# An early one-column activation on ScalarE and two new tables of order in a two-block kernel

## The chip, the cores and the metric

The kernel runs on one core of a Trainium2 chip. The metric is the device time of one execution in microseconds. The core has five engines, which run their own instruction streams and meet through semaphores: TensorE (PE: matmuls, and the loads of its stationary operand as PEld), VectorE (DVE), ScalarE (ACT), GpSimd (POOL) and SyncE (SP, which here only issues DMA transfers). ACT issues a few transfers too.

## The reference

256 tokens of width 1024, all in fp32, go through two blocks, one after the other, batch 1. Cut to what matters:

```python
# first block, on 16 meta tokens + 256 tokens (272 rows)
u = rmsnorm(h, g_pre_mix)
q, k, v, xr, yr = split(u @ w_in)
attn = sliding_window_attention_with_sinks(q, k, v, sinks)   # 8 heads, window 128
hr = rg_lru(causal_depthwise_conv(xr, conv_w, conv_b), ...)  # a gated linear recurrence
mix = concat([attn, gelu(yr) * hr]) @ w_out
h = h + rmsnorm(mix, g_post_mix)
u = rmsnorm(h, g_pre_ffn)
h = h + rmsnorm(square(relu(u @ w_ff1)) @ w_ff2, g_post_ffn)
# second block, on the 256 tokens
proj = rms_norm(h, ln_pre_mix) @ w_in_2                      # q, k, v, qkv_b, z, b, a, gates
y_a = moba_attention(rope(q), rope(k), v)                    # 8 heads of 128
y_b = rms_norm(gated_delta_rule(...)) * silu(z)              # 8 heads of 128
merged = sigmoid(gate_a) * (y_a @ w_proj_a) + sigmoid(gate_b) * (y_b @ w_proj_b)
h = h + rms_norm(merged @ w_out_2, ln_post_mix)
f = rms_norm(h, ln_pre_ffn)
h = h + rms_norm((silu(f @ w_ffn_gate) * (f @ w_ffn_up)) @ w_ffn_down, ln_post_ffn)
h = h + sigmoid(h @ w_ple_gate) * rms_norm(p @ w_ple, ln_ple)
```

The norms, attentions and recurrences are small. Most of the work is products with weight matrices, some 145 MB of them, each read once.

## The kernel before, in words

**Products in three.** A weight tile is 128 rows by 1024 columns of fp32, loaded by SP into a buffer called `raw` (four of them; `weight_dma`, L208). It is split in two halves of 512 columns (`prep`, L218 on): `whi` is the value rounded to the type that PE multiplies fast, `wlo` the rest, `raw` less `whi`. The activations are split the same way (`uT`, `mgT`, `hm`). A product is three matmuls, hi by hi, hi by lo and lo by hi (`mm3`). The rounding copy is one instruction on ACT or on DVE (`copy`: L174 on ACT, L172 on DVE), and the subtraction is one on DVE (L178). There are 258 weight tiles, so some 516 half splits. Groups of three matmuls follow one another on PE, and as long as the splits are ahead of them PE waits for nothing.

**The order of work.** Each engine runs its instructions in the order in which the Python code emits them. PE's matmuls are emitted by a list of jobs. Between groups of matmuls a job calls `tick()`, which counts steps and looks the number up in the table `ORDER_OF_WORK`: at that step a `p` emits one half split, and a name emits the next step of a generator of that name ("side"): `first` and `rest` are the splits and the x tiles of the start, `stats` and `rms` the first norm, `attn0` to `attn3`, `lru0` to `lru3` and `gdn0` to `gdn3` pieces of attention, recurrence and delta rule, `norm10` to `norm41` the norm boundaries between the parts (`norm30` and `norm31` for token rows 0 to 127 and 128 to 255 at the third of them). A second table, `VECTOR_COPIES`, lists for each stream (`m` for the jobs, `p12` for weight tile 12, or a side's name) which of its rounding copies go to DVE; the rest go to ACT. The two tables are data: no rule of the kernel derives them.

**The start.** DVE fills `warm`, `mhalf` and `ones` with constants (L540 to L542). PE multiplies `warm` with itself 20 times while the first transfers run. SP issues the first x tile (`xT`, four of them, two chunks of 128 features each) and the halves of the first two weight tiles; ACT issues `gc`, the gains of the first norm, 4 KB (L585). For each of eight chunks `x_prep` scales x by its gain on ACT (L576, the high part of `uT`) and takes the low part on DVE (L577). `part(i, j)` splits half j of weight tile i: (0,0) at once, then (1,0), (0,1) and (1,1) by the side `first`. The first job uses tiles 0 and 1: for each of the eight chunks three matmuls with tile 0 and three with tile 1, 48 in all.

**A norm boundary.** Each half (512 features) of the product in PSUM is squared and summed on ACT (L300), multiplied by the gain on DVE (`m`, L463), scaled by the norm and added to the residual `h` (L469). From `h` the next norm's `u` is made (L480), PE transposes it in blocks of 128 (L324), and ACT and DVE split the transposed half into two `uT` (L174, L178).

Of the kernel before, what the change touches and what calls it, by code (L numbers as in the profile page):

```python
# [56 lines left out]
10:stats,stats,p,stats,stats,p,stats,stats 11:p,stats,p 12:p 22:p 27:rms,rms 29:xr1*2 32:kv0*2,p,p 38:p,p 42:xr0*2
47:p 52:p,xr2*2 60:p 63:q0*2,xr3*2,p,p 64:p 73:lru1,lru2 77:kv1*2 78:attn0 80:lru0,lru1 81:vtok,attn1,lru3,lru3
86:attn0,p,lru1,p,p,p,p,p 87:attn1 90:q1*2 91:lru3 107:lru3 116:attn0 119:attn1 123:y0*2 125:attn2 126:lru3
132:attn0,attn3 133:rec0*2 135:p,rms 136:attn1,attn0*2 138:p 139:p,p 141:attn3 142:p,p,p 143:attn2,attn2 144:attn1*2  # L60
148:attn3 150:spill,y1*2 153:attn2 157:p,spill,attn2*2 166:p,p,p,p,p,p,attn3,p,p,rec1*2 171:rec0,attn3*2
173:p,p,p,rec1 182:p,p,p 192:p 196:p,p,p 202:norm10*2,p 204:norm10*2,norm10,norm10,norm10 208:norm11*2 212:norm10
218:norm11*2,norm11 219:norm10,norm10 221:norm11 224:p 226:norm11,norm11,norm11 228:norm11,p,p,p,p 235:p,p 244:p,p
254:p,p 257:hma0 261:hma1 279:p 281:p,p,p 285:p 295:p,p,p,p,p,p,p,p 319:p 340:p,p,p,p,p,p,p 342:spill 348:p,p 379:p,p
396:p 414:p,p,p,p,p,p 417:p,p,p,p,p 418:p 431:p,p 477:p 480:p 488:p,p,p,p,p,p,p 502:p 516:p 519:p,p 528:p,p,p,p,p,p
532:p 541:p,p 552:p 560:p 562:p,p 587:p,p,p 610:p 631:p,p,p,p,p 634:p,p,p,p,p 664:p,p,p 677:p 685:p,p 721:spill
729:p,p,p,p 732:p,p,p,p 735:p,p 739:p 766:p,p 783:p 789:p,p 803:p 811:p,p 820:p,p 833:p,p,p,p,p,p 849:p,p,p,p,p
871:norm20*2,norm20*2,norm20,norm20 873:norm20,norm20 875:norm21*2 883:norm20 885:norm21*2,norm21 886:norm20,norm21
894:p,norm21,p,norm21 896:p,p,norm21,norm21 900:p,p,p,gates 902:p,p,p,p 905:p,p,p 906:gates 910:p 911:p,p,p,p,p
912:gates 931:p,p,p,p 934:p,p,p 935:gates 940:p 964:p,p,p,p 979:p 992:p,p,p 1002:p,p 1019:p,p 1032:p,moba0 1050:moba1  # L70
1067:p 1068:p,p 1073:p,p 1076:moba1,moba1 1096:gates 1097:p 1100:p 1103:p 1107:moba0 1109:moba0 1110:moba2 1117:p
1125:p,moba1,p,p 1129:moba2 1136:moba2,moba0,moba1 1146:p,p,p 1164:p,p,p,moba3 1171:p,moba2 1191:moba3,moba3 1194:p
1195:p 1213:qkv01,qkv01 1220:p,p,p 1221:p 1223:qkv00,qkv00,qkv00,gates 1227:moba2,p 1233:qkv02,qkv02,gdn0
1243:p,gdn0,gdn0 1246:gdn0,gdn0,gdn0,gdn0,gdn0 1249:p,p,p,p 1259:p,p 1266:gdn0 1269:p 1273:p 1288:p 1292:p,p,p,p,p
1294:moba3 1314:p,p,p 1321:gdn0 1324:gdn0,p 1337:moba0,p 1354:qkv10,qkv10 1359:p,p,p,p,p 1366:gdn0,gdn0 1373:moba3
1379:qkv11,p 1389:p 1393:p,p 1396:qkv11 1405:gdn0 1406:gdn0,gdn0 1422:p,qkv10 1431:p,p,p 1434:qkv12
1435:qkv12,gdn1,gdn1 1440:gdn0 1441:gdn1,gdn1 1444:gdn0,gdn0,gdn1,gdn1 1454:p 1455:p,p,p 1460:qkv21 1466:gdn1
1467:gdn1 1468:gdn0 1484:qkv20,p,gdn0,qkv20,qkv20 1486:gdn0,gdn1 1487:p 1492:gdn1,gdn1,gdn0 1493:qkv22 1496:qkv30
1499:p 1502:gdn0 1503:qkv21 1506:qkv30,p 1515:gdn0 1516:qkv22,gdn2,gdn2 1520:p,gdn0,gdn1 1522:gdn1 1529:gdn0
1533:gdn2,gdn2 1535:qkv31 1536:p,p 1538:gdn0 1555:gdn0,gdn0 1559:qkv31,gdn2,gdn1,gdn1 1561:qkv30  # L80
1568:gdn0,qkv32,qkv32,gdn3,gdn3,gdn2,gdn2,gdn1 1575:p,p,gdn3,gdn2,gdn2,p,p,p,p 1584:p,gdn1 1587:gdn2 1593:gdn1,gdn1
1594:gdn3 1600:gdn1 1603:gdn1 1606:gdn3,gdn3 1607:p,p,p,p,p,p,gdn1,gdn2,gdn3,gdn2,gdn2 1616:gdn1 1627:gdn1 1632:gdn3
1633:gdn1 1639:gdn3,gdn1,p 1645:p,gdn1 1646:gdn2,gdn0,gdn2,gdn2 1658:gdn1 1669:p,p,p,p,p 1671:gdn2
1672:gdn3,p,p,p,gdn1,gdn3,gdn3,gdn3 1678:gdn1,gdn2,gdn2 1685:gdn0*2 1689:gdn1,gdn2 1691:p 1702:gdn2 1704:gdn1
1707:gdn3,gdn3,gdn3 1710:p,p,p,p 1715:gdn1*2,gdn3 1717:gdn2,gdn3,gdn2,p,gdn3 1720:p,gdn2 1731:gdn3 1734:gdn2
1741:p,p,p,p,gdn2 1743:gdn3,gdn2,p,p,p,p 1747:gdn3,p,p 1750:gdn2 1759:gdn3 1760:p 1769:gdn3,gdn2,gdn2 1773:gdn3
1779:gdn3 1783:gdn3 1789:gdn2 1792:gdn3 1793:p 1795:p,p 1796:gdn3 1802:gdn3 1809:gdn3 1811:gdn2,gdn3 1821:gdn2*2,p
1822:p 1825:gdn3*2 1827:p 1834:p,p 1840:p,p,p 1844:p 1848:p,p,p 1856:p 1863:p 1889:p 1909:p 1923:p,p 1932:pb1,pb0
1935:p,p,p 1936:p 1939:p 1942:p,p,pb2 1949:p 1967:p,p,p,p 1974:pb3,p 1976:p,p 1981:p,p 1996:p
2008:norm30*2,norm30*2,norm30,norm30 2018:norm30,norm31*2,norm30 2028:norm31*2,norm31 2029:norm30,norm30 2031:norm31  # L90
2034:p,norm31,norm31 2037:p,p,p,p,norm31,norm31,p,p,p 2047:p,p 2048:p 2054:p,p 2055:p 2056:p,p 2065:p,p 2073:hmb0
2074:hmb1 2081:p 2089:p 2093:p 2103:p 2110:p,p,p,p,p,p,p,p,p 2131:p,p,p,p 2140:p,p 2141:p 2150:p 2182:p,p
2217:p,p,p,p,p,p,p,p 2249:p,p 2252:p,ple 2281:p 2288:p,p,p,p,p 2300:p,p 2317:p,p,p 2319:p 2330:p,p,p 2332:p,p,p
2370:p,p,p,p 2376:p 2383:p,p,p 2392:p 2398:p 2402:p 2413:p,p,p,p 2421:p,p 2444:p,p,p,p 2485:p 2493:p 2501:p
2506:p,p,p,p,p,p 2545:p,p 2553:p,p 2564:p,ple,p,p,p,p 2597:p,p,p,p,p 2612:p,p,p,p 2615:p,p,p 2647:p,p 2654:ple
# [4 lines left out]
VECTOR_COPIES = """  # L100
m:0,2,4,5,8,10,12,13,16,17,18,19,21,23,24,26,27 first:2 p2:0,1 p3:0 p11:0 p14:1 p15:1 p16:0 p17:0,1 spill:0,1,3
attn1:3 attn2:0,1,2,3 p20:1 p27:1 p28:0 p30:1 hma0:1 p31:1 p32:0 p34:0 hma1:1 p35:0 p36:0 p37:1 p39:0 p40:0 p42:1
p43:1 p44:0 p46:0,1 p47:0 p49:1 p50:0 p51:0,1 p52:1 p53:0 p54:0 p55:0 p56:0,1 p57:0,1 p58:0,1 p59:0 p60:0,1 p61:1
p62:0 p63:0,1 p64:0,1 p65:0 p67:0 p68:0,1 p69:0 p70:1 p71:0,1 p73:1 p76:0 p77:0 p78:1 p79:1 p80:0,1 p81:1 p82:0 p83:1
p84:1 p85:0 p87:0,1 p88:0 p90:1 p91:1 p92:0 p95:0 gates:0,2,3 p98:0 p100:0,1 p103:0,1 p106:0 p107:1 p109:0 p110:0
moba0:1 p117:1 moba2:1 p122:0,1 p124:1 p126:0,1 p127:0 p129:1 p130:0 p132:1 p133:0 p134:1 p138:0 gdn0:2 p144:1 p145:0
p151:1 p152:0 p157:1 p159:1 gdn1:6 p162:1 gdn3:1,4 p163:1 p164:1 p165:0 p168:0 p169:1 p170:0 p171:1 p172:0,1 p173:1
p174:1 p177:1 p178:0,1 p179:1 p180:1 p181:1 pb3:0 p185:0,1 p187:0,1 p190:0,1 p191:0,1 p193:0,1 p194:0 p195:1 p196:0
hmb0:0 hmb1:1 p199:1 p200:0 p202:0 p205:0 p206:0 p207:1 p208:0 p209:0,1 p212:0,1 p213:0 p214:0 p217:0 p218:1 p219:0
p220:1 p221:1 p223:0 p224:0,1 p225:0,1 p226:0,1 p227:0,1 p229:1 p230:0,1 p232:1 p235:0,1 p238:1 p239:1 p240:1 p242:1  # L110
p243:1 p244:1 p245:1 p246:0,1 p247:1 p250:0 p252:0 p253:1 norm40:1 p256:0 norm41:0,1
"""


# [1394 lines left out]
```

## Time and profile before

| | |
|---|---|
| time, median of 3 runs | 847.17 us (847.0 to 847.31) |
| the profiled execution's own time | 847.02 us |
| its span (first to last instruction) | 845.2 us |
| PE busy | 837.2 us, 99% |
| DVE busy | 675.2 us, 80% |
| ACT busy | 362.6 us, 43% |
| POOL busy | 148.0 us, 18% |
| moved by DMA | 148.29 MB, mean 175 GB/s |

PE is busy nearly always. On DVE 516 subtractions of weights take 345.8 us, about half of its time. The profiled execution is shown in microseconds from the start of the span; the 1.8 us between span and time lie outside of it.

### The profile page before, as it was taken

The page shows a single profiled execution, that of the slowest core. Times are in us where ns is not written, and L with a number is a line of the kernel's source. Part 1 is how long each engine was busy: PE and PEld are TensorE (multiplying, and loading weights), DVE is VectorE, ACT ScalarE, POOL GpSimd, SP SyncE. Part 2 cuts the span into 40 slices and gives each one's busy share as a digit, 9 for nine tenths or more (in the row PEclk, how much of TensorE's full clock was granted, in tenths as well). Part 3 has the DMA queues.
Part 4 walks back from the last instruction along what each step waited for, and adds up shares of the span by engine and source line. Part 5 has one row for each costly group of instructions (what it writes and reads, how often), then busy time and mean ns, then how long its engine had stood idle before and what let it go on. Part 6 is the DMA issues. An engine that isn't in the chain of part 4 may idle for free.

```text
span 845.2 us, 15349 instructions
## 1 busy us (share of the span) xinstructions
PE 837.2 (99%) x5883; PEld 772.2 (91%) x5883; DVE 675.2 (80%) x1296; ACT 362.6 (43%) x841; POOL 148.0 (18%) x242
## 2 busy tenths in 40 slices
...
GB/s 341 169 99 239 195 150 264 205 184 236 217 190 197 85 237 210 126 134 117 207 149 104 79 106 191 103 157 156 205 151 194 239 236 197 196 253 153 198 100 51
DMA packets 48778, 148.29 MB, mean 175 GB/s; under 512 B 9521, under 2 KB 10801, under 8 KB 48705
## 3 DMA queue, kind: packets, MB, share of 16 engines
...
q14 instruction: 28, 0.22, 0.1%
q10 hardware_dynamic: 288, 0.07, 0.0%
HBM read 144.93 MB, written 2.36 MB: 174 GB/s over the span
## 4 chain that ended last, share of the span: by engine, by line
PE 93%; ACT 3%; DVE 2%; DMA 1%; issue 0%; SPq 0%; ACTq 0%; DVEq 0%
PE ps L161 91%; PE ps L183 1%; DVE wlo L178 1%; PE ps L324 1%; DMA xT<-in_xT 1%; DVE g L776 0%; ACT g L523 0%; ACT g L788 0%; ACT g L774 0%; ACT g L790 0%; ACT g L789 0%; DVE g L663 0%; ACT g L514 0%; PE ps L1011 0%; ACT whi L174 0%
## 5 line engine op out<-in xcount | busy, mean ns | idle before, releaser
L161 PE MATMUL ps<-uT,whi 128*128 128x256 f32 (+1 forms) x2272 | 417.9, 285 | 0.9 <-DVE whi L172 0.7
L178 DVE TENSOR_TENSOR wlo<-raw,whi 128x512 fp32r<-128x512 f32 x516 | 345.8, 706 | 19.3 <-ACT whi L174 11.6
L161 PEld LDWEIGHTS ps<-uT,whi 128*128 128x128 f32 x2272 | 351.7, 189 | 5.7 <-issue 1.2
L161 PE MATMUL ps<-uT,wlo 128*128 128x256 f32 (+1 forms) x1136 | 319.9, 282 | 0.7 <-DVE wlo L178 0.6
L174 ACT ACTIVATE whi<-raw 128x512 fp32r<-128x512 f32 x331 | 190.2, 624 | 148.9 <-DMA raw<-in_ff 43.7
L161 PEld LDWEIGHTS ps<-uT,wlo 128*128 128x128 f32 x1136 | 215.4, 190 | 1.4 <-DVE wlo L178 1.4
L161 PE MATMUL ps<-whi,hm 128*128 128x512 f32 x432 | 139.0, 394 | 0.0
L161 PEld LDWEIGHTS ps<-whi,hm 128*128 128x128 f32 x432 | 81.3, 188 | 17.4
L161 PE MATMUL ps<-wlo,hm 128*128 128x512 f32 x216 | 85.0, 394 | 0.0
L172 DVE CAST whi<-raw 128x512 fp32r<-128x512 f32 x185 | 80.3, 434 | 4.1 <-DMA raw<-in_ff 3.3
L161 PE MATMUL ps<-whi,uT 128*128 128x512 f32 (+1 forms) x256 | 74.6, 370 | 0.8 <-ACT uT L174 0.5
L161 PE MATMUL ps<-g 128*128 128x128 f32 (+9 forms) x560 | 74.1, 279 | 0.4 <-ACT g L174 0.4
L305 POOL TENSOR_TENSOR ms<-ms,mhalf 128x1 f32<-128x1 f32 (+1 forms) x19 | 10.7, 565 | 362.1 <-DVE ms L304 362.1
L161 PEld LDWEIGHTS ps<-g 128*128 128x128 f32 (+5 forms) x560 | 62.7, 176 | 6.5 <-issue 2.8
L161 PEld LDWEIGHTS ps<-whi,uT 128*128 128x128 f32 x256 | 45.7, 188 | 10.7 <-DVE uT L178 1.7
L161 PEld LDWEIGHTS ps<-wlo,hm 128*128 128x128 f32 x216 | 40.6, 188 | 8.3
L161 PE MATMUL ps<-wlo,uT 128*128 128x512 f32 (+1 forms) x128 | 46.9, 367 | 0.0
L1090 DVE SCALAR_TENSOR_TENSOR g<-ps,vec,g 128x255 f32<-128x255 f32 (+2 forms) x72 | 29.1, 472 | 3.3 <-ACT g L1086 3.1
L174 ACT ACTIVATE g<-ps 128x256 f32<-128x256 f32 (+3 forms) x38 | 14.8, 411 | 38.0 <-PE ps L161 30.1
L161 PEld LDWEIGHTS ps<-wlo,uT 128*128 128x128 f32 x128 | 24.1, 188 | 3.8
L932 ACT ACTIVATE g<-ps 128x512 f32<-128x512 f32 x14 | 8.3, 593 | 40.6 <-PE ps L161 40.5
L933 DVE TENSOR_TENSOR g<-g 128x512 f32<-128x512 f32 x14 | 9.6, 688 | 18.8 <-ACT g L932 18.8
(236 smaller groups left out, 914.7 us busy)
## 6 DMA issues: line engine op xcount, KB each, us to landing
...
```

Source lines behind the costliest of these rows:

```text
L161: pe.matmul(o, lhsT=l, rhs=r, start=start, stop=stop)
L172: dve.tensor_copy(dst, src)
L174: act.activation(dst, src, AF.Copy)
L178: (eng or dve).tensor_tensor(lo, src, hi.bitcast(F32), op=SUB)
L183: pe.transpose(ps[:, blk(j)], src[:, blk(j)], ident)
L305: pool.tensor_tensor(ms[:r, 1:2], ms[:r, 0:1], mhalf[:r, 0:1], op=ALU.pow)
L324: pe.transpose(ps[:, k, :r], us[j][:, blk(k)], ident[:r, :r])
L932: act.activation(r, ps, AF.Relu)
L933: dve.tensor_tensor(r, r, r, op=MUL)
L1090: dve.scalar_tensor_tensor(xc[:, o + s:o + T], in0=ps[:, o:o + T - s], scalar=V("conv2", col[m] - s), in1=xc[:, o + s:o + T], op0=MUL, op1 ...
```

## The change

The change has two parts. The first adds two lines after the constants: a tile of one column, and an activation (Tanh) from `ones` into it. Nothing reads the result. ACT's first activation is preceded by the load of its function table, so the load now belongs to this one. The second part replaces both tables of numbers. PE's matmuls and their order of jobs are the same; which splits and which side steps are emitted at which tick is different, and so is which rounding copies go to DVE (185 casts of weights before and after). Line numbers behind the two tables are 2 higher, and 4 higher behind the added lines.

```diff
@@ -53,62 +53,64 @@
 ORDER_OF_WORK = """
-1:rest,first,rest,rest,first,first,rest,rest,rest,rest 2:p 3:stats,stats,stats 4:p 6:stats,stats
+1:rest,first,rest,rest,rest,first,first,rest,rest,rest,p 2:stats,stats,stats 3:p 8:stats,stats
...
 VECTOR_COPIES = """
-m:0,2,4,5,8,10,12,13,16,17,18,19,21,23,24,26,27 first:2 p2:0,1 p3:0 p11:0 p14:1 p15:1 p16:0 p17:0,1 spill:0,1,3
+m:0,1,2,4,5,9,10,13,16,17,18,19,21,23,24,26,27 first:0,1 p2:0 p3:0 p14:1 p15:1 p16:0 p17:0,1 spill:0,1,3 attn1:3
...
@@ -540,6 +542,8 @@
     dve.memset(warm, 1.0)
     dve.memset(mhalf, -0.5)
     dve.memset(ones, 1.0)
+    early = small("early", (P, 1))
+    act.activation(early, ones, AF.Tanh)
```

The start of ACT's program, before. `uT_110` is the high part of x, `whi` a rounded half of a weight:

```order
L585 DMA gc<-in_gc 128x8
L576 ACT_TABLE_LOAD
L576 ACTIVATE uT_110<-xT,gc 128x272 x2
L174 ACTIVATE whi<-raw 128x512
L576 ACTIVATE uT_110<-xT,gc 128x272 x2
```

And now:

```order
L546 ACT_TABLE_LOAD
L546 ACTIVATE early<-ones 128x1
L589 DMA gc<-in_gc 128x8
L580 ACTIVATE uT_112<-xT,gc 128x272 x5
L176 ACTIVATE whi<-raw 128x512
```

The table load and the new activation stand ahead of the transfer of `gc`, and five scalings of x now come ahead of ACT's first copy of a weight, where two did. The matching start of DVE's program, before (`uT_111` is the low part of x):

```order
L577 SCALAR_TENSOR_TENSOR uT_111<-xT,gc,uT_110 128x272
L172 CAST whi<-raw 128x512
L178 TENSOR_TENSOR wlo<-raw,whi 128x512
L577 SCALAR_TENSOR_TENSOR uT_111<-xT,gc,uT_110 128x272
L178 TENSOR_TENSOR wlo<-raw,whi 128x512
```

And now:

```order
L581 SCALAR_TENSOR_TENSOR uT_113<-xT,gc,uT_112 128x272
L174 CAST whi<-raw 128x512
L180 TENSOR_TENSOR wlo<-raw,whi 128x512
L581 SCALAR_TENSOR_TENSOR uT_113<-xT,gc,uT_112 128x272
L174 CAST whi<-raw 128x512
L180 TENSOR_TENSOR wlo<-raw,whi 128x512
```

The second rounding copy, of tile 1's first half, came from ACT before and stands on DVE now. DVE's program at the first attention's denominators (`s_m`; the long steps on 544 columns belong to the recurrence), before:

```order
L796 SCALAR_TENSOR_TENSOR g<-g 128x544
L516 TENSOR_TENSOR s_m<-s_m,bcv 128x4
L172 CAST whi<-raw 128x512
L178 TENSOR_TENSOR wlo<-raw,whi 128x512
L798 SCALAR_TENSOR_TENSOR g<-g 128x544
L178 TENSOR_TENSOR wlo<-raw,whi 128x512 x5
```

And now:

```order
L180 TENSOR_TENSOR wlo<-raw,whi 128x512 x2
L518 TENSOR_TENSOR s_m<-s_m,bcv 128x4
L800 SCALAR_TENSOR_TENSOR g<-g 128x544
L802 SCALAR_TENSOR_TENSOR g<-g 128x544
L800 SCALAR_TENSOR_TENSOR g<-g 128x544
L180 TENSOR_TENSOR wlo<-raw,whi 128x512 x4
```

The split of weight tile 11 stood behind the denominator of `attn0` and stands in front of it now. PE's program at the third norm boundary, before (`mgT` is the merged activation, `uT_7635` and `uT_7636` the transposed `u` of token rows 0 to 127):

```order
L161 MATMUL ps<-wlo,mgT 128x512
L161 MATMUL ps<-whi,mgT 128x512
L324 MATMUL ps<-ident,u 128x128 x8
L161 MATMUL ps<-whi,uT_7635 128x512
L161 MATMUL ps<-wlo,uT_7635 128x512
```

And now:

```order
L326 MATMUL ps<-ident,u 128x128 x4
L163 MATMUL ps<-whi,mgT 128x512
L163 MATMUL ps<-wlo,mgT 128x512
L163 MATMUL ps<-whi,mgT 128x512
L326 MATMUL ps<-ident,u 128x128 x4
L163 MATMUL ps<-whi,uT_7630 128x512
```

The eight transposes are parted in two fours with three matmuls between them. At the last norm boundary DVE's program has, in front of the last residual (L469, now L471), a row of rounding casts and subtractions of two weight tiles that stood behind it before; the transposes of that residual on PE stand nine matmuls later.

## Rows read from the trace of the kernel before

**Rows 1.** Busy times of the page: us, share of the span, instructions.

```profile
PE 837.2 (99%) x5883; PEld 772.2 (91%) x5883; DVE 675.2 (80%) x1296; ACT 362.6 (43%) x841; POOL 148.0 (18%) x242
```

**Rows 2.** What PE waited for, all of the span: us, times, longest.

```profile
PE ps L161 <- DVE whi L172: 0.7, 1, 0.7
...
PE ps L161 <- ACT uT L174: 0.5, 1, 0.5
```

**Rows 3.** Stretches at the start: us, busy (instructions) of PE, PEld, DVE, ACT, POOL, PEclk, DMA, GB/s.

```profile
6.00:7.00 1.00, 0.49 (x2) 0.30 (x2) 0.97 (x3) 0.93 (x2) 0.00 (x0) 1.00 1.03 376
...
9.00:10.00 1.00, 1.00 (x7) 1.00 (x6) 0.96 (x3) 0.29 (x1) 0.00 (x0) 0.50 1.03 351
...
12.00:14.00 2.00, 2.00 (x17) 2.00 (x16) 1.39 (x5) 0.76 (x4) 0.00 (x0) 0.91 1.04 396
```

**Rows 4.** ACT at the start: start, us, line, operation, [idle before, releaser].

```profile
0.72 0.40 ACTq L585 DMA_DIRECT2D gc<-in_gc  x1
3.56 1.28 ACT L576 ACT_TABLE_LOAD   x1 [3.56 <-DMA xT<-in_xT]
4.86 0.93 ACT L576 ACTIVATE uT<-xT,gc 128x272 fp32r<-128x272 f32 x2
```

**Rows 5.** DVE at the start, same columns.

```profile
5.41 0.50 DVE L577 SCALAR_TENSOR_TENSOR uT<-xT,gc,uT 128x272 fp32r<-128x272 f32 x1 [4.41 <-ACT uT L576]
5.83 0.42 DVE L172 CAST whi<-raw 128x512 fp32r<-128x512 f32 x1
6.29 0.69 DVE L178 TENSOR_TENSOR wlo<-raw,whi 128x512 fp32r<-128x512 f32 x1
6.89 0.50 DVE L577 SCALAR_TENSOR_TENSOR uT<-xT,gc,uT 128x272 fp32r<-128x272 f32 x1
```

**Rows 6.** PE at the start, same columns.

```profile
1.04 4.63 PE L161 MATMUL ps<-warm 128*128 128x128 f32 x20 [1.04 <-DVE ones L542]
6.40 0.49 PE L161 MATMUL ps<-uT,whi 128*128 128x272 f32 x2 [0.73 <-DVE whi L172]
...
9.08 0.65 PE L161 MATMUL ps<-uT,whi 128*128 128x272 f32 x2
...
12.44 0.41 PE L161 MATMUL ps<-uT,whi 128*128 128x272 f32 x2
...
14.95 0.29 PE L161 MATMUL ps<-uT,wlo 128*128 128x272 f32 x1
```

**Rows 7.** DMA issues of the first 2 us: KB, median us to landing.

```profile
gc<-in_gc ACTq DMA_DIRECT2D x1, 4.0 KB, 3.0
```

**Rows 8.** ACT behind the second norm boundary, columns of rows 4.

```profile
294.22 0.33 ACTq L951 DMA_DIRECT2D g<-in_wba  x1
294.27 0.59 ACT L174 ACTIVATE uT<-ps 128x512 fp32r<-128x512 f32 x1
```

**Rows 9.** DVE and PE at the first attention's denominator, columns of rows 4.

```profile
48.19 0.17 DVE L516 TENSOR_TENSOR s_m<-s_m,bcv 128x4 f32<-128x4 f32 x1 [0.45 <-ACT g L514]
...
48.33 0.28 PE L161 MATMUL ps<-uT,wlo 128*128 128x256 f32 x1
...
49.47 0.38 PE L161 MATMUL ps<-uT,wlo 128*128 128x256 f32 x1 [0.22 <-DVE wlo L178]
```

**Rows 10.** PE and ACT at the third norm boundary, columns of rows 4.

```profile
626.84 1.03 PE L324 MATMUL ps<-ident,u 128*128 128x128 f32 x8
...
627.68 1.08 ACT L174 ACTIVATE uT<-ps 128x512 fp32r<-128x512 f32 x2
...
628.32 0.50 PE L161 MATMUL ps<-whi,uT 128*128 128x512 f32 x1 [0.45 <-ACT uT L174]
...
629.23 0.73 PE L161 MATMUL ps<-whi,uT 128*128 128x512 f32 x2 [0.17 <-DVE uT L178]
```

**Rows 11.** DVE and PE at the last norm boundary, columns of rows 4.

```profile
820.05 1.42 DVE L469 SCALAR_TENSOR_TENSOR h<-m,ms,h 128x512 f32<-128x512 f32 x2 [0.73 <-POOL ms L305]
...
823.15 0.60 PE L324 MATMUL ps<-ident,h 128*128 128x128 f32 x4
```

More of the change, by code (lines that the diff above doesn't have):

```diff
@@ L55 @@
 ORDER_OF_WORK = """
-1:rest,first,rest,rest,first,first,rest,rest,rest,rest 2:p 3:stats,stats,stats 4:p 6:stats,stats
[L57 to L95, printed above, removed]
@@ L96 @@
-2673:p,p,p 2678:p 2687:ple 2699:p 2707:p,p 2709:p,p,p 2713:norm40*2,norm40*2,norm40,norm40 2717:norm41*2,norm40,norm40
-2721:p 2723:p 2725:norm41*2 2730:norm41,norm41 2734:p,p,norm41 2735:norm41 2747:p,p,p 2757:p
+1:rest,first,rest,rest,rest,first,first,rest,rest,rest,p 2:stats,stats,stats 3:p 8:stats,stats 9:stats,stats
+10:p,stats,stats,stats 12:stats,p 14:p 17:stats 19:p 22:p,p 27:rms,rms 29:xr1*2 37:p,p,p,xr2*2 38:p,p,p,p 45:kv0*2
+48:p 54:xr0*2 57:p,p 64:lru1 70:q0*2 74:xr3*2,lru2,lru0,kv1*2 77:attn0,attn1 80:lru3,vtok 84:p,p 86:attn0
@@ new lines @@
+90:lru1,lru1,lru3,p,p,p,p 91:attn1 99:q1*2,lru3 110:lru3,attn0 115:attn1 120:y0*2 125:attn2,lru3,rec0*2 130:attn3
+135:attn0,rms,attn1 136:p,p,attn0*2 138:p 142:p 145:attn3 147:p,p,p 148:attn2,attn2 150:spill,attn3 151:y1*2,attn1*2
+153:attn2 155:p,spill 157:attn2*2 160:p,p,p,p 164:p,p,attn3,rec1*2,rec1,p,p 169:attn3*2 173:rec0,p,p 180:p 186:p
+192:p,p,p,p,norm10*2,p 202:p 204:p,norm10*2,norm10,norm10,p 210:norm10 212:norm11*2 216:norm10 218:norm11*2,norm11
+219:norm10,norm10,norm11 222:norm11,norm11 226:norm11 228:norm11 233:p,p,p,p 237:hma0 247:p,p,p,p,p 251:hma1 252:p
@@ new lines @@
+255:p,p,p 264:p 266:p,p 279:p,p,p 296:p 310:p 312:p,p,p 314:p 326:p 330:p 339:p,p 342:p,p,p 348:p 358:p,p
+390:p,spill,p,p 402:p,p 407:p,p,p,p,p,p,p 440:p 444:p 457:p,p,p 471:p,p,p,p,p 474:p,p,p 490:p,p 509:p 511:p 528:p
+532:p,p,p 543:p 547:p,p,p,p,p 565:p 581:p,p,p 590:p 622:p,p 625:p 633:spill 654:p,p 656:p,p 657:p 660:p 666:p 679:p
+681:p 682:p,p,p,p 684:p 715:p,p,p,p,p 736:p,p,p,p,p,p,p 759:p 763:p 767:p,p 775:p,p 813:p,p,p,p,p,p,p 855:p
+861:p,p,p,p,p,p 875:norm20*2,norm20*2,norm20,norm20,norm20,norm20,norm21*2 883:norm20 885:norm21*2,norm21 886:norm20
@@ new lines @@
+887:norm21 888:p 889:norm21 891:p 894:norm21 896:p,p,norm21,norm21 897:p 900:p,p 901:p,p,p,p 902:p 903:p 905:gates
+906:p 907:p,p,p 909:p 910:p 915:gates 916:p,p,p 920:p 921:gates 922:gates 938:p,p 943:p 954:p,p 963:p,p 967:p,p
+995:p,p,p 1012:moba0 1018:p 1021:p,moba0,moba0 1039:p 1041:p 1042:moba0,p,p,p,p 1054:moba1 1061:p,p 1064:moba1 1065:p
+1068:moba1 1080:gates 1083:p 1091:p,p 1094:p,p 1099:p 1119:p 1136:moba2,moba1 1154:moba1 1159:moba2,moba2 1164:moba3
+1165:gates,p,p,p 1181:p 1182:p,p 1184:qkv00,qkv00 1188:p,qkv00 1200:qkv01,qkv01 1203:p,p,p,p 1213:p,p 1220:qkv02
@@ new lines @@
+1227:qkv02,gdn0,gdn0 1230:gdn0 1232:p 1243:p 1246:p,p 1247:gdn0 1249:p,p 1250:gdn0 1255:p,p 1262:p 1268:moba3
+1286:moba3 1291:p,p,p,moba2 1294:p,p,p,p 1307:gdn0,p,gdn0 1310:p,p 1311:gdn0,gdn0 1315:gdn0,gdn0 1317:gdn0 1324:p
+1343:p 1356:p,qkv10 1357:qkv10 1363:p,gdn0,p,p 1366:moba3 1367:moba2 1372:moba0 1380:qkv11,qkv11 1389:moba3,p
+1393:qkv12 1399:p,p 1405:p 1408:gdn0,gdn0 1421:p,p 1424:gdn0 1434:qkv10,qkv12,gdn1 1437:p,gdn1 1441:gdn1 1442:gdn0
+1444:gdn1,qkv21 1448:p,gdn0 1450:gdn0 1460:gdn1,p,p,p 1461:gdn1,gdn1 1467:gdn0 1470:qkv21
@@ new lines @@
+1471:p,p,gdn0,qkv20,qkv20,qkv20 1474:gdn1 1481:p 1484:p 1489:gdn1 1492:gdn0 1500:gdn0 1502:p 1507:gdn1
+1509:qkv22,qkv22,gdn0,gdn1 1515:p,p,gdn0,p,gdn2,gdn2 1518:gdn1 1519:qkv30 1520:gdn0 1526:gdn0 1528:gdn1
+1533:qkv30,gdn2,gdn2 1538:gdn0,p,p 1539:qkv31 1544:gdn0 1545:qkv31 1559:gdn2,gdn1,gdn1 1564:gdn0,gdn0
+1568:qkv30,qkv32,qkv32,gdn1,gdn3,gdn3,gdn2,gdn2 1577:gdn1,p,p,p 1581:p 1584:gdn1,gdn1 1585:gdn2,gdn3,gdn2,gdn2
+1594:gdn3,p,gdn1 1600:gdn1 1603:gdn3,p,gdn1,gdn3 1604:p,p 1610:p,gdn1 1614:gdn1 1616:p
@@ new lines @@
+1620:gdn3,gdn0,gdn1,gdn2,gdn2,gdn2 1624:p,p 1633:gdn1 1640:p 1643:p 1648:gdn2,gdn1,gdn2 1653:gdn2
+1655:gdn3,gdn3,gdn3,gdn3 1659:gdn1 1662:p,p,p 1665:gdn2,p,p 1672:gdn2,gdn2,p,p,gdn1 1675:gdn0*2 1676:gdn2
+1685:gdn3,gdn3 1698:gdn1,gdn1 1701:p 1707:gdn2 1711:gdn1 1714:gdn3,gdn3,gdn2,gdn3 1715:p,p 1718:gdn3,gdn1*2 1720:gdn3
+1721:gdn3 1723:gdn2,p 1727:gdn2 1728:p,p,gdn3 1733:gdn2,gdn3 1736:p,p 1740:gdn2 1741:p 1744:p,gdn2 1747:p,p,gdn3,p,p
+1752:p,gdn2 1756:gdn3 1760:gdn3 1767:p,p 1769:gdn2,gdn3,gdn2,gdn2 1776:gdn3 1778:p 1785:gdn3 1792:gdn3
@@ new lines @@
+1795:gdn3,gdn3,gdn2,gdn3 1811:p 1814:gdn3 1822:p,p,p 1824:gdn2*2,p,gdn3*2,p 1840:p,p,p,p,p,p,p,p 1857:p,p,p 1879:p
+1883:p 1909:pb0 1918:p,p 1931:p 1945:p,p,p,p 1958:p,p 1961:pb1 1965:p,p,pb3 1976:p,pb2,p 1990:p,p,p,p,p,p 1994:p,p,p
+2008:norm30*2,norm30*2,norm30,norm30,norm30 2014:norm30 2018:norm31*2 2026:norm30 2028:norm31*2,norm31 2029:norm30
+2032:norm31,norm31,norm31,p 2034:p 2036:p 2037:p,norm31,norm31 2038:p 2046:p 2054:p,p 2055:p,p,p 2059:p 2065:p
+2070:p,p 2074:p 2080:hmb0 2081:p 2093:p,p,p 2097:p 2104:hmb1,p,p,p,p,p,p,p,p,p,p,p 2133:p,p 2159:p,p 2167:p,p,p,p,p
@@ new lines @@
+2180:p,p 2229:p 2239:p 2243:p,p,p 2253:p 2271:p 2280:p,p 2291:p,p,p,p,p,p 2306:ple 2322:p,p,p,p,p,p,p,p,p 2337:p,p
+2370:p 2376:p,p,p 2384:p,p,p,p,p,p 2387:p 2398:p 2441:p,p,p,p 2443:p 2449:p 2460:p,p 2466:ple,p 2500:p 2501:p,p,p
+2503:ple 2504:p 2510:p,p 2513:p,p 2519:p 2530:p,p 2538:p,p,p 2553:p 2561:p 2574:p,p 2577:p,p 2580:p 2621:p
+2624:p,p,p,p 2627:p 2654:p,p 2656:p,p,p 2685:p,p 2697:ple,p,p,norm40*2,p,p 2707:p 2715:p,norm40*2,norm40,norm40
+2717:p,p,norm41*2,norm40,norm40 2727:norm41*2,norm41,p 2728:p,p 2733:norm41 2737:norm41,norm41 2743:p 2747:p 2757:p
@@ L98 @@
+2762:p
 """
 VECTOR_COPIES = """
-m:0,2,4,5,8,10,12,13,16,17,18,19,21,23,24,26,27 first:2 p2:0,1 p3:0 p11:0 p14:1 p15:1 p16:0 p17:0,1 spill:0,1,3
[L102 to L110, printed above, removed]
```

11 lines of the change are left out of this document (10 added, 1 removed).

## The prediction, made before the changed kernel was run

> **What bounds the kernel now.** I read the page's busy times first: PE is busy for 837.2 us, 99% of the span of 845.2 [rows 1], so only the last 8 us can be won without removing matmuls, and the change removes none. The list of what PE waits for came second. Its entries that depend on the order of work are fractions of a microsecond: 0.7 for the first cast of a weight, 0.5 for a copy of the transposed activations on ACT [rows 2]. I therefore went to the places in time. [...] The timelines of ACT, DVE and PE at the start, and of the few places where PE waits later, came last.
>
> **The start, part one: the table.** In the row of before ACT issues the small load of gc at 0.72; its table load starts only at 3.56, when the first xT tile is there, and lasts 1.28; the first scaling of x starts at 4.86 [rows 4]. gc lands 3.0 after its issue [rows 7], at 3.7. So the table load is what ends last there, by 1.1 us. In the changed kernel the load stands first, with nothing to wait for, and the one-column activation behind it waits for the column of ones, which PE also waits for and gets at 1.04 [rows 6]. The load of gc now stands behind that activation. If ACT's queue goes on as soon as the activation's wait is met, gc is issued at about 1.05 and lands at 1.05 + 3.0 = 4.05, and that is now what is late: x is scaled at 4.05 instead of 4.86, 0.81 earlier. That the queue does go on is seen later in the same trace: a load on ACT's queue (L951) stands in program order behind both copies into uT, and is issued at 294.22, before the second of them starts at 294.27 [rows 8]. The activation itself (one column) has 2 us in which nothing else is on ACT, and costs nothing.
>
> **The start, part two: DVE.** The operands of PE come from DVE. There a low half of x takes 0.42 to the next start, a cast 0.46, a low half of a weight 0.60, and the first low half of x starts 0.55 after ACT's scaling (5.41 less 4.86) [rows 4, 5]. The new list puts the second weight's cast on DVE too, so its train is x, cast, low, x, cast, low: from 4.05 the starts are 4.60, 5.02, 5.48, 6.08, 6.50 and 6.96. The last of these is the low half of weight 1, which PE needs for its sixth matmul; before it started after x, cast, low, x without the second cast, 6.89 + 0.42 = 7.31. Of the 0.81, the added cast takes 0.46 back, and 0.35 remain. Does that reach the end of the first job? Matmul 13 starts at 9.08 and 28 at 12.44, so 15 take 3.36 at the low clock (0.224 each); 28 to 48 take 2.51, or 0.1255 each [rows 6]. If the clock falls and returns at the same times, three matmuls more are done beforehand, and 3 x 0.1255 = 0.38 is saved, which agrees with 0.35. I take **−0.35**. The bounds: +0.8, if gc is late (below), and −1.83, if the clock does not fall.
>
> **Weight 11 behind the first attention.** At 48.19 DVE starts the attention's denominator, having waited for ACT; the split of a weight's half stands behind it. PE goes from its matmul at 48.33 to the one at 49.47, three matmuls, in 1.14 [rows 9]; unhindered, 256 columns take 0.118 each by the 0.1255 of 272 columns, so 0.36, and 0.78 is lost. In the new list both subtractions of the split stand ahead of that denominator. Nothing else on DVE there holds them, so I take all of it, **−0.78**; the denominator comes later by two subtractions, 1.2, and the matmuls that want the attention are far behind. Bounds: 0, if the next weight is late instead by as much, and −0.78.
>
> **The third norm boundary.** Before, eight transposes run in one go at 626.84; ACT copies the two halves from 627.68, PE gets its first operand at 628.32 after 0.45 idle and the next at 629.23 after 0.17 [rows 10]. Eight transposes keep PE busy some 0.86 (1.03 less the tail), and took 1.48 to the next start; two 512-column matmuls take 0.47 (0.1255 x 512/272 = 0.236 each) and took 0.91; so 0.62 + 0.44 = 1.06 is lost. The new order is four transposes, three matmuls (0.7 us of work), then four more, and on ACT and DVE each half is copied and subtracted as soon as it is there. The first half's copy then lies beside those matmuls. I take **−0.9**: 0.7 of matmuls cover ACT's copy, and the subtraction of the second half may still show. Bounds −1.06 and 0.
>
> **Everything else in the two lists.** About 500 half-weight splits move by some places. Between these places the splits keep at least 19 matmul groups ahead of their use in the new list, and the number of casts on DVE stays 185. I cost this at nothing but for two thin places, weight 12 (now behind the recurrence's steps) and the last norm boundary: **+0.2**, about a quarter of the loss at weight 11. There DVE now has two casts and three subtractions in front of the last residual: 2 x 0.46 + 3 x 0.60 = 2.7. The residual ended at 820.05 + 1.42 = 821.47 and its transposes started at 823.15 [rows 11], a reserve of 1.68; in the new order the transposes stand nine matmuls later on PE, about 1.1, so 2.8 stands against 2.7. It just fits. Bounds 0 and +2.7.
>
> **The sum.** Against the profiled execution's own 847.02 (0.15 below the median of the runs): 847.02 − 0.35 − 0.78 − 0.9 + 0.2 = 845.2, and with the 0.15, **845.3**.
>
> **The rivals.**
> 1. The clock does not fall at 9 us. For it: PE is fed at once after the warming matmuls, which end at 1.04 + 4.63 = 5.67, without the 0.73 of idle that follows them [rows 6]. Against: PE is still fed at DVE's pace, some 15 matmuls of 0.12 in the 3.4 us up to 9, against 12 before, and the busy share of [rows 3] would rise only from about a half. It saves 15 x (0.224 − 0.1255) = 1.48 more: 843.9.
> 2. gc comes late. If ACT's queue stands until the activation has run, gc is issued after the table load, at about 0.7 + 1.28 + 0.2 = 2.2, lands at 5.2, and x is scaled 0.34 later than before; with the cast that is now on DVE, 0.34 + 0.46 = 0.8 later at the sixth matmul. Then 845.3 + 0.35 + 0.8 = 846.5. For it: ACT's queue is in order and the load of gc was moved behind the activation. Against: [rows 8].
>    [...]
> 3. The last norm boundary decides, on the slow side: DVE's 2.7 us of splits in front of the last residual are not covered. PE's transposes stand in order, and everything behind them waits. From a reserve below 0.9 instead of 2.8 all of the gain is gone. At the full price it is 845.3 + 2.7 = 848.0, slower than before; with rival 2 849.2. For it: the sum above fits by 0.1 only. Against: before, DVE idled there for 0.73 on POOL, which the added work fills.
> 4. The order's two gains don't come, since the next weight in line is as late as the one that was helped: 845.3 + 0.78 + 0.9 = 847.0.
>
> **How the numbers follow.** Forecast 0.42; rival 1 0.24; rival 2 0.15; rival 3 0.12; rival 4 0.07. A measurement of this kernel can tell 0.2%, 1.7 us, from no change, so faster means below 845.5, slower above 848.9. The forecast's own range, 844.5 to 846.1, lies on that edge: a bit over half of its chance, 0.25, is faster, with nearly all of rival 1 (0.23) and a little of rival 2, where the clock gives some of it back (0.05): 0.53. Slower is that part of rival 3 in which gc is late too or the stall grows: 0.09. Same is the rest, 0.38. The range: 843.5 leaves out a part of rival 1, 847.3 most of rival 3: 843.5 to 847.3.
>
> **What would show it.** In the profile after: the table load before 1 us, gc issued close to 1.05 (right) or after 2 (rival 2), the first scaling of x at about 4.05, the sixth matmul at about 7.7 against 8.05. The clock's row of 9 to 10 us at 0.50 (forecast) or 1.00 (rival 1). At 47 to 49 and at 625 to 628 us PE without a wait for weight 11's low half and for uT. Around 820 us no idle time in front of the transposes of the last residual. The forecast is wrong if the matmuls of the first job end later than 14.95, or if any single new wait of PE is over a microsecond.

## The result, and the profile after

The changed kernel takes 842.61 us (median of 4, 842.25 to 843.86) against 847.10 for the one before: a ratio of 0.995, interval 0.9935 to 0.9966. It is faster, by 4.5 us where 1.8 was forecast, and the time lies below the range. The span of the profiled execution went from 845.2 to 841.0.

The page's busy times, answering to [rows 1]:

```profile
PE 833.6 (99%) x5883; PEld 768.9 (91%) x5883; DVE 678.3 (81%) x1301; ACT 360.0 (43%) x837; POOL 147.7 (18%) x242
```

PE is busy 3.6 us less, with the same 5883 matmuls. That is the first sign of what the prediction missed: most of the gain isn't waiting time. (A matmul at the lower clock counts as busy: from 9 to 10 us PE was busy throughout with 7 matmuls at a clock of 0.50 [rows 3] and is so now with 11 at 1.00. So a part of the 3.6 is the stretch of before at 0.50.) What PE waited for (us in total, times, longest), answering to [rows 2]:

```profile
PE ps L326 <- DVE u L482: 0.8, 2, 0.6
PE ps L163 <- ACT g L176: 0.8, 1, 0.8
PE ps L163 <- DVE wlo L180: 0.4, 2, 0.2
PE ps L163 <- DVE whi L174: 0.2, 1, 0.2
```

The waits for the first cast of a weight and for the copies into uT are all but gone; 0.8 for u and 0.8 for a copy on ACT stand in their place.

The start, by stretch, as in [rows 3]:

```profile
6.00:7.00 1.00, 0.76 (x4) 0.54 (x3) 0.97 (x3) 0.49 (x2) 0.00 (x0) 1.00 1.01 382
9.00:10.00 1.00, 1.00 (x11) 1.00 (x10) 0.97 (x3) 0.85 (x3) 0.00 (x0) 1.00 1.00 308
12.00:14.00 2.00, 1.80 (x15) 1.57 (x13) 1.27 (x4) 1.33 (x5) 0.00 (x1) 1.00 1.05 400
```

The clock column reads 1.00 from 9 to 10 us, where it read 0.50. ACT there, in the columns of [rows 4]:

```profile
0.72 1.28 ACT L546 ACT_TABLE_LOAD   x1 [0.72 <-PEq L1503]
1.05 0.41 ACTq L589 DMA_DIRECT2D gc<-in_gc  x1
2.01 0.20 ACT L546 ACTIVATE early<-ones 128x1 f32<-128x1 f32 x1
3.82 0.93 ACT L580 ACTIVATE uT<-xT,gc 128x272 fp32r<-128x272 f32 x2 [1.61 <-DMA gc<-in_gc]
```

The table load runs at 0.72, gc is issued at 1.05 while the load still runs, and x is scaled at 3.82. DVE's train, in the columns of [rows 5]:

```profile
4.38 0.50 DVE L581 SCALAR_TENSOR_TENSOR uT<-xT,gc,uT 128x272 fp32r<-128x272 f32 x1 [3.37 <-ACT uT L580]
4.80 0.42 DVE L174 CAST whi<-raw 128x512 fp32r<-128x512 f32 x1
5.25 0.69 DVE L180 TENSOR_TENSOR wlo<-raw,whi 128x512 fp32r<-128x512 f32 x1
5.86 0.50 DVE L581 SCALAR_TENSOR_TENSOR uT<-xT,gc,uT 128x272 fp32r<-128x272 f32 x1
6.27 0.42 DVE L174 CAST whi<-raw 128x512 fp32r<-128x512 f32 x1
6.72 0.69 DVE L180 TENSOR_TENSOR wlo<-raw,whi 128x512 fp32r<-128x512 f32 x1
```

It is the foretold one, 0.2 earlier: gc landed 2.7 us after its issue, where 3.0 had been reckoned with. PE, answering to [rows 6]:

```profile
1.04 4.64 PE L163 MATMUL ps<-warm 128*128 128x128 f32 x20 [1.04 <-DVE ones L544]
5.36 0.79 PE L163 MATMUL ps<-uT,whi 128*128 128x272 f32 x2
...
7.47 0.39 PE L163 MATMUL ps<-uT,wlo 128*128 128x272 f32 x1 [0.21 <-DVE wlo L180]
...
9.09 0.28 PE L163 MATMUL ps<-uT,wlo 128*128 128x272 f32 x1
...
13.15 0.29 PE L163 MATMUL ps<-uT,wlo 128*128 128x272 f32 x1
```

The sixth matmul is the row at 7.47, the 48th the row at 13.15; it was at 14.95. The first attention, the rows that answer to [rows 9]:

```profile
45.13 1.27 DVE L180 TENSOR_TENSOR wlo<-raw,whi 128x512 fp32r<-128x512 f32 x2
...
46.33 0.14 DVE L518 TENSOR_TENSOR s_m<-s_m,bcv 128x4 f32<-128x4 f32 x1
...
46.94 0.28 PE L163 MATMUL ps<-uT,wlo 128*128 128x256 f32 x1
...
47.29 0.28 PE L163 MATMUL ps<-uT,wlo 128*128 128x256 f32 x1
```

Both subtractions of the split stand before the denominator, and from 46.94 to 47.29 three matmuls take 0.35. Later in the attention, and at the first norm boundary, stand the two new waits:

```profile
57.93 0.28 PE L163 MATMUL ps<-uT,wlo 128*128 128x256 f32 x1
58.96 0.43 PE L163 MATMUL ps<-g 16*64 16x128 f32 x2 [0.75 <-ACT g L176]
```

```profile
99.34 0.40 PE L163 MATMUL ps<-whi,mixT 128*128 128x512 f32 x1
100.35 0.63 PE L326 MATMUL ps<-ident,u 128*128 128x128 f32 x4 [0.61 <-DVE u L482]
```

The third norm boundary, answering to [rows 10]:

```profile
622.43 1.41 DVE L482 SCALAR_TENSOR_TENSOR u<-h,ms,gain 128x512 f32<-128x512 f32 x2 [0.67 <-POOL ms L307]
...
623.33 0.63 PE L326 MATMUL ps<-ident,u 128*128 128x128 f32 x4
...
624.49 0.60 PE L326 MATMUL ps<-ident,u 128*128 128x128 f32 x4
...
624.84 0.48 PE L163 MATMUL ps<-whi,uT 128*128 128x512 f32 x1
...
625.40 0.70 PE L163 MATMUL ps<-whi,uT 128*128 128x512 f32 x2
```

Neither four waits for much, and the uT matmuls follow at once. The last boundary, answering to [rows 11]:

```profile
817.75 1.41 DVE L471 SCALAR_TENSOR_TENSOR h<-m,ms,h 128x512 f32<-128x512 f32 x2
```

```profile
820.00 1.04 PE L326 MATMUL ps<-ident,h 128*128 128x128 f32 x8
```

The last residual ends at 817.75 + 1.41 = 819.16 and its transposes start at 820.00: a reserve of 0.84, no wait. Before, DVE had waited 0.73 for POOL in front of this residual [rows 11]; the row above carries no wait, so the added splits filled that idle time.

To see where the 4.2 us of span went I compared the starts of the same matmuls of the weight jobs. At 22 us the changed kernel is 1.27 earlier, at 99 us 2.28, at 110 us 1.86, at 640 us 3.38, at 800 us 4.17. Between 640 and 840 us, where PE waits for nothing in either trace, 0.8 is gained. There the matmul itself is quicker: the 256-column matmuls that stream uT start 118.69 ns apart before and 118.04 after (mean over some 3200 of each behind 22 us, gaps of 150 ns and more left out). Those that stream yaT, the transposed y_a of the second block, are a check: its tiles start at a multiple of 64 bytes in both programs, and the pace is 118.37 before and 118.38 after. The 512-column ones that stream a weight are equal within 0.3 ns in 231.

### The profile page after: what moved, and what is told of

The parts are those of the page before. It is cut to its first block, busy times and chain, and to the rows that moved or that the text cites. A ratio compares the mean times of both kernels' runs of the same rounds, so it can differ in the third digit from the quotient of the medians.

```text
span 841.0 us, 15347 instructions
## 1 busy us (share of the span) xinstructions
PE 833.6 (99%) x5883; PEld 768.9 (91%) x5883; DVE 678.3 (81%) x1301; ACT 360.0 (43%) x837; POOL 147.7 (18%) x242
## 4 chain that ended last, share of the span: by engine, by line
PE 90%; DVE 4%; ACT 2%; DMA 2%; issue 1%; POOL 0%; SPq 0%; ACTq 0%; DVEq 0%
PE ps L163 88%; DVE wlo L180 2%; PE ps L185 1%; PE ps L326 1%; DMA raw<-in_ff1t 1%; DMA raw<-in_w1in 1%; DMA xT<-in_xT 1%; ACT whi L176 1%; ACT junk L302 0%; DVE g L780 0%; ACT g L525 0%; DVE s_m L511 0%; ACT g L778 0%; DVE g L667 0%; DVE m L465 0%
## 5 line engine op out<-in xcount | busy, mean ns | idle before, releaser
L163 PE MATMUL ps<-g 128*128 128x128 f32 (+8 forms) x560 | 73.3, 278 | 0.8 <-ACT g L176 0.8
L1197 POOL TENSOR_TENSOR tmp<-g 32x14 f32<-32x14 f32 (+6 forms) x56 | 25.1, 448 | 14.0 <-DMA g<-sc 10.3
```

Source lines behind the costliest of these rows:

```text
L163: pe.matmul(o, lhsT=l, rhs=r, start=start, stop=stop)
L1197: pool.tensor_tensor(tmp, w[:, 0:j, j:j + 1].to_broadcast([32, j, 15 - j]), w[:, j:j + 1, j + 1:].to_broadcast([32, j, 15 - j]), op=MUL)
```

## The experiments

Two theories for what was missed. **Place:** the added one-column tile takes 32 bytes of each partition in front of most small tiles and of the two uT tiles. In the built program uT starts at byte 202,976 before and 203,008 after; the first is 32 more than a multiple of 64, the second is one. **Start:** the early table load does more than bring x earlier, it keeps the clock up. The rival to both: the new order of work does it all. The kernel before was timed anew beside each group of experiments: 846.82, 846.97 and 846.88.

**One part of the change at a time.** The tables of before with the activation:

```diff
     dve.memset(ones, 1.0)
+    early = small("early", (P, 1))
+    act.activation(early, ones, AF.Tanh)
```

> The tables of before, and of the change only the one-column activation with its table load. Start theory (the early table load alone keeps the clock up): PE's granted clock stays at 1.00 from 5 to 14 us, the 48th matmul of the first job is over 1 us earlier than the 14.95 of before, and the rest of the trace keeps its distance: about 845.8. Address theory (the one-column tile moves the two uT tiles by 32 bytes, and each 256-column matmul that streams uT then takes 0.5 ns less, 1.9 us in all): the pace of these matmuls after 22 us falls from 118.7 to 118.2 ns and the time is 843.9. Rival, the order of work: nearly all of the 4.5 us comes from the tables, and this kernel takes 846.5 or more.

Measured: 844.26, ratio 0.9971 (0.9958 to 0.9983). The pace is 118.07 ns, the clock does not fall in the profiled execution, the 48th matmul starts at 13.42, and the distance to the trace of before grows from 1.24 at 22 us to 3.05 at 840. The signs of both theories are there; more than half of the gain comes without any new order.

Both new tables without those two lines:

> Both new tables, without the one-column activation and its tile. Start theory: the table load waits for the first x tile again, the clock falls at about 9 us; address theory: the pace of the 256-column matmuls stays at 118.7 ns. Both together: only the new order's own gains and losses are left (weight 11 -0.9, third norm boundary -0.6, first norm boundary +0.4, attention's transposes +0.4), so 846.4. Rival, the order of work: 843 to 844.

Measured: 846.89, ratio 1.0 (0.9992 to 1.0009); pace 118.70 ns, the clock falls (at 9.5 us), the 48th matmul at 15.45, later than before. The new order alone is worth nothing that can be measured.

**The place alone.** One edit in the kernel before, no instruction added or moved:

```diff
-    gc = small("gc", (P, KD))
+    gc = small("gc", (P, 2 * KD))[:, :KD]
```

> The kernel before with one edit: the tile of gc is allocated 64 bytes wide instead of 32, the added half unused. No instruction is added or moved; every tile behind it, the two uT among them, moves by 32 bytes. Address theory: 256-column matmuls that stream uT at 118.2 ns instead of 118.7, time 845.2. Rivals (the order, or a chance of the single profile): 118.7 ns and 847.1.

Measured: 844.65, ratio 0.9974 (0.9964 to 0.9984), pace 118.06 ns. The same edit in the changed kernel, which puts uT at 32 beyond a multiple of 64 again:

> The changed kernel with the tile of gc 64 bytes wide, so that the uT tiles lie 64 bytes behind their place in the kernel before, 32 behind that of the changed one. Address theory: the pace is that of before again, 118.7 ns, and the time 844.5. Rivals: 118.2 ns and 842.6.

Measured: 845.27, ratio to before 0.9982 (0.9973 to 0.9991), pace 118.74 ns: 2.7 us of the gain are taken back. Then the tile was singled out, with unused bytes in front of and behind uT, so that only uT moves within 64 bytes:

```diff
-    ... hgn = ... small("hgn", (P, 1))
+    ... hgn = ... small("hgn", (P, 16))[:, :1]
...
-        return [hp.tile([P, KD, TM], F32R, tag=f"uT{i}", name=f"uT{i}") for i in range(2)]
+        t = [hp.tile([P, KD, TM], F32R, tag=f"uT{i}", name=f"uT{i}") for i in range(2)]
+        small("spare", (P, 1))
+        return t
```

> The kernel before, with 32 unused bytes in front of the two uT tiles and 32 behind them, so that of all tiles only uT changes its place within 64 bytes. No instruction differs. If it is uT's place: 256-column matmuls that stream uT at 118.1 ns instead of 118.7, 844.7 us. If it is another tile's (the small ones of the norms and attention): 118.7 ns and 847.

And the second half of that edit alone, so that uT stays and all behind it moves:

> The kernel before, with 32 unused bytes behind the uT tiles: uT stays, all smaller tiles behind it move by 32 bytes. If it is uT's place: 118.7 ns and 847, as before. If it is one of the tiles behind it: 118.1 ns and 844.7.

Measured: 844.66, ratio 0.9973 (0.9962 to 0.9983), pace 118.03 ns; and 846.93, ratio 1.0001 (0.9992 to 1.001), pace 118.69 ns. Of the tiles that moved, it is uT. In the built programs the first of these two edits changes the place within 64 bytes of the two uT tiles and of no other tile, the second that of six small tiles behind them. The same two matmuls show it in PE's timeline. First the kernel before, then gc widened, then uT moved alone, then the tiles behind uT moved:

```profile
200.09 0.40 PE L161 MATMUL ps<-uT,whi 128*128 128x256 f32 x2
...
800.21 0.39 PE L161 MATMUL ps<-wlo,hm 128*128 128x512 f32 x1
```

```profile
199.55 0.40 PE L161 MATMUL ps<-uT,whi 128*128 128x256 f32 x2
...
797.83 0.39 PE L161 MATMUL ps<-wlo,hm 128*128 128x512 f32 x1
```

```profile
198.74 0.40 PE L161 MATMUL ps<-uT,whi 128*128 128x256 f32 x2
...
796.98 0.39 PE L161 MATMUL ps<-wlo,hm 128*128 128x512 f32 x1
```

```profile
199.61 0.40 PE L161 MATMUL ps<-uT,whi 128*128 128x256 f32 x2
...
799.73 0.39 PE L161 MATMUL ps<-wlo,hm 128*128 128x512 f32 x1
```

From the first row to the second it is 600.12, 598.28, 598.24 and 600.12 us. All four run the same instructions, the clock is at 1.00 throughout, and PE waits 0.6 us in each, at the third norm boundary; so the 1.8 to 1.9 us are paid in the pace.

**The start alone.** The first experiment with 6 warming products instead of 10, so that PE stands idle before its first operands, and the third with 13, to fill the idle time there:

```diff
-WARM = 10
+WARM = 6
```

> The kernel of the first experiment (tables of before, early activation) with 6 warming products instead of 10, so that PE stands idle from about 3.6 us until its first operands at 5.4. Clock theory (what the early load is worth at the start is that PE goes on at once after the warming matmuls, so the clock does not fall): the clock falls, the 100th matmul that streams uT is at 22.2 or later instead of 21.2, and the time is 845.3. Operand theory (it is worth the 0.8 us by which the operands come earlier): 21.2 and 844.2.

> The kernel of the third experiment (late table load, uT moved) with 13 warming products instead of 10, so that PE has work until its first operands at 6.5. Clock theory: the clock does not fall, the 100th matmul that streams uT is at 21.4 instead of 22.1, and the time is 843.8. Operand theory: the operands come no earlier, 22.2 and 844.7.

Measured: 844.61 and 844.79. In the traces both came out as the clock theory says: the 100th matmul that streams uT starts at 22.41 (21.18 with 10 products) and at 21.30 (22.12 with 10). Ahead of its first operand PE idles 1.35 with 6 and still 0.62 with 13, where the third experiment had 0.81. PE with 6 products:

```profile
1.04 2.93 PE L161 MATMUL ps<-warm 128*128 128x128 f32 x12 [1.04 <-DVE ones L542]
5.32 0.79 PE L161 MATMUL ps<-uT,whi 128*128 128x272 f32 x2 [1.35 <-DVE whi L172]
...
8.04 0.65 PE L161 MATMUL ps<-uT,whi 128*128 128x272 f32 x2
...
8.72 0.65 PE L161 MATMUL ps<-uT,whi 128*128 128x272 f32 x2
```

From 8.04 to 8.72 three matmuls take 0.68, 0.227 each, the pace of the lower clock (0.224 each before from 9.08 to 12.44), though PE waits for no operand there. But the times moved by +0.35 and +0.14 where +1.0 and −0.9 were expected, so the clock theory's price is not confirmed by them. The two profiled executions are not typical: the one with 6 products is the second slowest of its eight, the one with 13 the fastest of its seven. The trace of the experiment with uT alone moved says more: it has the late table load and 10 products, and its clock did not fall either (100th matmul at 21.29). So the program does not fix whether it falls. Each execution's mean granted clock tells how often at the least: with the late load it is 0.998 or lower in 52 of 101 executions (all runs of before beside the experiments, and the four experiments with its table load and 10 products), with the early load and 10 products in 2 of 47, with 6 products in 2 of 8, with 13 in none of 7. These counts are too low where the trace's record of the clock begins late: in the profiled execution with gc widened the first matmuls run at half the pace up to 10.6 us (three take 0.68 from 8.53 to 9.21) and the record begins only there, so its mean reads 1.00; the one with 6 products reads 0.999.

The same numbers price the clock in the times. Of the 64 executions of before, the 32 with a mean of 0.998 or lower have a median of 847.01, the others 846.49; with gc widened it is 845.16 against 844.54. That is some 0.5 to 0.6 us, and more if some of the others started slowly without a record of it; it is less than the 0.8 and 1.2 us between the pairs of traces above.

**Two terms of the order.** On the first experiment, only weight 11's split moved ahead of the denominator:

```diff
-86:attn0,p,lru1,p,p,p,p,p
+84:p,p 86:attn0,lru1,p,p,p,p
```

> The kernel of the first experiment (tables of before, early activation), with one edit of the order: weight 11's half split is emitted ahead of the first attention's denominator instead of behind it. Theory (the term of the prediction, -0.78, measured as -0.9 with the whole table): the matmuls behind 50 us are 0.8 to 0.9 earlier than in the first experiment and keep this lead to the end: 843.4 against 844.26. Rival (the next weight is late instead): the lead is gone by 55 us, 844.2.

Measured: 845.15, 0.9 above the first experiment's 844.26; their ratios to before, 0.9979 (0.997 to 0.9988) and 0.9971 (0.9958 to 0.9983), are not told apart, so what follows rests on the two traces. The lead is 0.62 at 50 us, gone at 55, and by 58 us the kernel has lost 0.6, and this stays to the end. DVE and PE there:

```profile
46.74 1.29 DVE L178 TENSOR_TENSOR wlo<-raw,whi 128x512 fp32r<-128x512 f32 x2
...
47.95 0.16 DVE L516 TENSOR_TENSOR s_m<-s_m,bcv 128x4 f32<-128x4 f32 x1
...
52.26 0.16 DVE L516 TENSOR_TENSOR s_m<-s_m,bcv 128x4 f32<-128x4 f32 x1 [0.85 <-ACT g L514]
52.34 0.68 DVE L667 TENSOR_TENSOR g<-ps,rB 128x512 f32<-128x512 f32 x1
...
53.07 0.39 PE L161 MATMUL ps<-g 64*128 64x144 f32 x2 [0.58 <-DVE g L667]
```

The denominator now waits for the split: it starts at 47.95, in the first experiment at 46.94. Through ACT the second one comes at 52.26 (51.77), the product behind it at 52.34, and PE's attention matmuls wait 0.58 for it. The rival is right for this move by itself: the lead does not last. In the changed kernel the attention's and recurrence's steps in front of it were moved too.

The new tables at the third norm boundary alone:

> The kernel of the first experiment with the new tables only for the third norm boundary and the matmul groups around it (steps 1890 to 2243 of the list, where as many splits are emitted at both ends). Theory (the prediction's -0.9; the trace of the changed kernel suggests -0.6): matmuls behind 640 us are 0.6 earlier than in the first experiment: 843.7. Rival (a new wait at the transposes takes as much): 0 and 844.2.

Measured: 843.80 (five runs, 843.59 to 845.18), 0.5 under the first experiment; the ratio to before, 0.9967 (0.9955 to 0.998), is not told apart from that one's either. The profiled execution is the slowest of the five, and in it the boundary costs 0.6 more than in the first experiment, not less: ACT waits for a weight, DVE is late with u, and the first four transposes wait for it.

```profile
614.10 0.63 ACT L123 ACTIVATE whi<-raw 128x512 fp32r<-128x512 f32 x1 [5.46 <-DMA raw<-in_ffgt]
```

```profile
624.43 1.42 DVE L429 SCALAR_TENSOR_TENSOR u<-h,ms,gain 128x512 f32<-128x512 f32 x2 [0.67 <-POOL ms L254]
...
625.33 0.63 PE L273 MATMUL ps<-ident,u 128*128 128x128 f32 x4 [1.01 <-DVE u L429]
```

In the last experiment below, which has the same steps there, ACT waits less for the same weight, and the boundary gains 0.3:

```profile
611.31 0.63 ACT L123 ACTIVATE whi<-raw 128x512 fp32r<-128x512 f32 x1 [4.01 <-DMA raw<-in_ffgt]
```

By these two traces the boundary's gain hangs on when a weight lands, and is not there in every execution.

**Two more.** The changed kernel with gc issued ahead of the activation:

```diff
+    act.dma_start(gc, a["gc"])
     act.activation(early, ones, AF.Tanh)
```

> The changed kernel with the transfer of gc issued ahead of the early activation. gc is issued at 0.72 instead of 1.05 and the first scaling of x starts 0.1 to 0.3 earlier, with the first x tile. If the operands' start decides: the 100th matmul that streams uT is at 20.9 instead of 21.15, time 842.3. If the later weight loads decide (PE waits for a weight at 13.4 us in the changed kernel): 21.15, and 842.6.

Measured: 842.76, ratio to before 0.9957 (0.9944 to 0.9969). x is scaled at 3.76 instead of 3.82, the 100th matmul is at 21.43: nothing gained, so the place of gc behind the activation costs nothing that shows.

The new tables in two sections only, the first attention and the third norm boundary, on the first experiment:

> The kernel of the first experiment with the new tables in two sections: the first attention (steps 30 to 99) and the third norm boundary (steps 1890 to 2243). It leaves out the sections of the new tables in which the changed kernel loses against the first experiment (first norm boundary +0.2, the weights between 110 and 290 us +0.4). Theory (the order's gains are local and add up): -1.1 by 70 us and -0.6 at 640 us against the first experiment, 842.5, and a span under the 841.0 of the changed kernel. Rival (the sections' gains are given back later): 843.5 or more.

Measured: 842.52 (842.27 to 843.36), ratio to before 0.9953 (0.9939 to 0.9966), span 840.5. It equals the changed kernel; the intervals do not tell the two apart. In the traces it is ahead of the first experiment by 0.35 at 22 us, where both have the same program, by 1.41 at 70, 1.61 at 640 and 1.75 at the end. So 1.06 of the order's 1.4 lie in the first attention.

## Why the prediction was wrong

The sign was right, the size was not. The step that failed is the first one: PE is busy for 837.2 us, "so only the last 8 us can be won without removing matmuls". The matmuls are the same 5883, and most of what was won was won inside the busy time. With it failed the step on the added lines, "the activation itself (one column) ... costs nothing". The prediction priced each instruction and no allocation, so its sum has no term for the tile. The tile moves uT by 32 bytes, and some 3290 matmuls that stream 256 columns of uT take 0.65 ns less each: 2.1 us in the trace, 2.2 to 2.3 in the times (experiments with gc widened and with uT alone), 2.7 when taken back from the changed kernel.

The changed kernel with uT put back to 32 beyond a multiple of 64 takes 845.27; the forecast was 845.3. So the place is about all that the sum lacked. That the rest came out is in part luck, since its terms were off one by one:

- **The start, −0.35; measured −1.27** at 22 us. The steps came as foretold: gc was issued at 1.05 behind the activation's wait, so ACT's queue did go on, and rival 2 is out; the sixth matmul came at 7.47, foretold 7.7. What came out otherwise is the clock: rival 1, given 0.24, is what the profile shows (1.00 from 9 to 10 us). It cannot be priced from one execution, since before the clock fell in about half of them or more. On the median the early load with the old tables is worth 0.4 (844.26 against 844.65), which lies within the spread of the runs; the term of 0.35 is near it, but the 1.48 of rival 1 is not borne out.
- **Weight 11, −0.78; measured −0.9** at that place, and then partly given back: the new wait on ACT at 58 us is 0.36 longer than the one before. By itself, with the old steps around it, the move gains nothing. The step that was wrong is that the denominator may come 1.2 later since "the matmuls that want the attention are far behind": they came to wait 0.58 for it.
- **Third norm boundary, −0.9; measured −0.5** between 620 and 640 us. Its own experiment has −0.5 in the times, not clear of the spread, and +0.6 in the trace.
- **Everything else, +0.2.** The first norm boundary loses 0.4 (0.61 of waiting for u). Against the first experiment's trace, which has uT in the same place, the changed kernel loses another 0.7 between 110 and 600 us and wins 0.4 behind 640. Some 0.3 of the 0.7 lies in 192 matmuls between 579 and 602 us, which stream ybT, the transposed y_b: they start 119.98 ns apart instead of 118.59, with the tables alone too (119.97). Its tiles start at multiples of 64 in all three, so this is not the place; why stays open. Rival 3 did not happen: the reserve at the last boundary stayed at 0.84 where 0.1 was worked out, because the splits filled the time in which DVE had idled; the prediction had named that as the argument against this rival.

The experiments also show that the parts do not add. The tables are worth nothing without the early load (846.89 against 846.82) and 1.65 with it (842.61 against 844.26; 1.2 in the two traces). Of the traces' difference 0.5 is the start, where the new list with the late load makes the 100th matmul 0.5 later than the old one (22.92 against 22.42). The rest, some 0.7, comes behind 600 us. Counted from 22 us, both pairs of traces gain the same up to there (0.03 without the early load, 0.09 with it); then it is 0.29 against 0.70 from 600 to 640 us, the third norm boundary, and 0.15 against 0.37 from there to the end. Why stays open.
